# Feed-forward layers and second mixer: 2x2 block products with seven block multiplications, acts through DRAM

## The chip, the cores and the metric

The kernel runs on one core of one Trainium2 chip. The metric is the device time of one execution in microseconds (us). A profiled execution is known by its span, from its first to its last instruction. PE is the matrix engine, DVE the vector engine, ACT the scalar engine, POOL the GpSimd engine, SP the queue that issues the DMAs. PSUM is the memory that PE writes (8 banks of 512 float32 numbers per partition, a tile here is two banks), SBUF the working memory.

## The reference

Two layers on x of 1024 tokens by 1024 channels, float32. What concerns the change is what follows the first mixer: a gated feed-forward layer, the second mixer (a short convolution between two gates), and a second feed-forward layer.

```python
def mixer_c(h, w_in, conv_w, conv_b, w_out):          # w_in 1024 x 3072, w_out 1024 x 1024
    bg, cg, v = jnp.split(h @ w_in, 3, axis=-1)
    return (bg * causal_dwconv(cg * v, conv_w, conv_b)) @ w_out

def conv_ffn(h, w_gate, w_up, conv_w, conv_b, w_down): # w_gate, w_up 1024 x 2816, w_down 2816 x 1024
    g = causal_dwconv(h @ w_gate, conv_w, conv_b)      # 3 taps over the tokens
    return (jax.nn.silu(g) * (h @ w_up)) @ w_down
# around each: h = rms_norm(x, g_pre) * (1 + sc) + sh ;  x = x + (1 + gm) * rms_norm(y, g_post)
```

The vectors sc, sh and gm come from `mod = silu(c) @ mod_w[i] + mod_b[i]`, whose weights stream through the kernel too.

## The kernel before

Every product is done in three passes of a shortened float32 format: an operand x is kept as hi + lo, and a product is hi·hi + hi·lo + lo·hi. A pass over a 128x128 stationary tile and 512 moving columns is one matmul.

*Stages.* First the first mixer (recurrence and attention), to about 1177 us. Then `rest` (L1226): feed-forward layer 0, the second mixer, feed-forward layer 1. All weights come as units of 128x1024 in one fixed stream (L58) through three SBUF buffers `w_st`; `w_pump` (L172) splits each into `w_hi` (ACT cast, L209) and `w_lo` (two POOL subtractions of 512 columns, L211 through the helper at L146), five units deep. Units of `mod_w` are not split: DVE adds each into a sum (L249).

*Up products.* `proj` (L332) multiplies one unit (128 output features, 8 tiles of 128 input channels) with h^T, kept as `hh` and `hl` for two halves of 512 tokens: 8 x 3 x 2 = 48 matmuls into a two-bank PSUM tile. A feed-forward feature tile takes two units, gate and up; `gate_post` (L1302) makes the three-tap convolution (ACT L1306, two DVE operations L1308 that read PSUM), Silu (L1309), the product with up (L1311) and the split of the act (ACT L367, POOL L146). The second mixer takes three units for each tile of 128 channels.

*Output products.* After two feature tiles a `chunk` (L1246) multiplies their acts with two units of the output weights: for each of 8 token tiles 2 x 3 x 2 = 12 matmuls (`down`, L343), and DVE adds PSUM into y (L359). So up and output products alternate. The last chunk (L1279) takes four feature tiles, 24 matmuls for a token tile; each token tile is followed by `bnd1` (L301): two norms (ACT squares, POOL power L298), the residual on DVE (L308, L309), the store, and y normed on ACT (L313).

*Between layers.* `to_h` (L315) transposes y on PE (L321), applies the modulation (DVE L323) and splits h (ACT L325, then POOL or DVE L329 in turn). One half of the tokens is made inside the last chunk; `pre_half` (L1259) then runs the first two units on that half, 48 matmuls, while the other half is made.

*Order.* Each engine runs its instructions in one fixed order. It is set at build by a planner that starts from the written order and a modelled timeline (L1495); the trace shows transposes and products of different units put between each other at the layer borders.

Of the kernel before, what the change touches and what calls it, by code (L numbers as in the profile page):

```python
# [57 lines left out]
def _unit_order():  # L58
# [24 lines left out]
    def ffn(i, mods):  # L83
        for c in range(NF // 2 + 1):
            if c < NF // 2:
                for f in (2 * c, 2 * c + 1):
                    order.extend([("fg", i, f), ("fu", i, f)])
                    if mods:
                        order.append(mods.pop(0))
            if c == NF // 2:  # L90
                order.extend(mods)
                order.extend(("fd", i, f) for f in range(NF - 4, NF))
            elif 0 < c < NF // 2 - 1:
                order.extend([("fd", i, 2 * c - 2), ("fd", i, 2 * c - 1)])
                if mods:
                    order.append(mods.pop(0))
# [3 lines left out]
    for c in range(5):  # L100
        if c < 4:
            for j in (2 * c, 2 * c + 1):
                for k in (1, 2, 0):
                    order.append(("sc", 8 * k + j))
                    if mods:
                        order.append(mods.pop(0))
        if c in (1, 2):
            order.extend([("sco", 2 * c - 2), ("sco", 2 * c - 1)])
        if c == 4:
            order.extend(("sco", j) for j in range(4, 8))  # L110
# [11 lines left out]
def _is_raw(u):  # L122
    return u[0] in ("mod", "modk", "lru")
# [6 lines left out]
class K:  # L130
# [6 lines left out]
    # ------------------------------------------------------------ helpers  # L137
# [13 lines left out]
    # ------------------------------------------------------------ weight stream  # L151
# [20 lines left out]
    def w_pump(self, ahead):  # L172
        """issue loads and splits up to `ahead` units past the next one to be used"""
        upto = min(len(UNITS), self.w_next + ahead)
        while True:
# [12 lines left out]
            while self.w_split_n < upto and self.w_split_n < self.w_dma_n:  # L188
# [8 lines left out]
                hi = self.p_w.tile([128, 1024], FR, name="w_hi", bufs=self.nw)  # L197
                lo = self.p_w.tile([128, 1024], FR, name="w_lo", bufs=self.nw)
# [64 lines left out]
    def mods_here(self, limit=99):  # L263
        """the modulation units that come next in the stream"""
# [36 lines left out]
    def bnd1(self, tt, rowG, src, dst, x, last=False):  # L301
        """the residual after a layer, x = src + rstd(y) y G, goes to dst; y becomes rstd(x) x"""
# [3 lines left out]
        y = self.y[:, tt, :]  # L306
# [8 lines left out]
    def to_h(self, src, half, A, B, tmp, ks=range(8)):  # L315
        """h^T (hi, lo) of 4 token tiles from their normed tiles src(tt): A and B are columns"""
        nc = self.nc
        for k in ks:
            ps = self.ps1()
            for q in range(4):  # L320
                nc.tensor.transpose(ps[:, q * 128:(q + 1) * 128], src(4 * half + q)[:, k * 128:(k + 1) * 128], self.ident)  # L321
            hf = tmp()
            nc.vector.tensor_scalar(hf, ps, A[:, k:k + 1], B[:, k:k + 1], op0=OP.mult, op1=OP.add)  # L323
            hh, hl = self.hh[half][:, k, :], self.hl[half][:, k, :]
            nc.scalar.copy(hh, hf)  # L325
            if k % 2:
                self.pool_sub(hl, hf, hh.bitcast(FT))
            else:
                nc.vector.tensor_tensor(hl, hf, hh.bitcast(FT), op=OP.subtract)  # L329
# [13 lines left out]
    def down(self, tt, ws, acts, ps):  # L343
        """ps[:, half, :] = sum over the chunk's feature tiles of a^T[:, tt]^T W"""
        n, last = 0, 3 * len(ws) - 1
        s = slice(tt * 128, (tt + 1) * 128)
        for (ah, al), (hi, lo) in zip(acts, ws):
            for st, mv in ((ah, hi), (ah, lo), (al, hi)):
                for h in range(2):
                    self.nc.tensor.matmul(ps[:, h, :], st[:, s], mv[:, 4 * h:4 * h + 4, :],  # L350
                                          start=(n == 0), stop=(n == last))
                n += 1

    def y_add(self, tt, ps):
        nc = self.nc
        y = self.y[:, tt, :]
# [1142 lines left out]
```

## Time and profile before

| | |
|---|---|
| three runs | 3044.17, 3044.5, 3047.75 us; median 3044.5 |
| profiled execution | span 3045.4 us; no other time of its own is given |
| mean granted TensorE clock | 0.978 of full speed |
| PE busy | 2887.9 us, 95% of the span, 13329 matmuls |
| DVE, ACT, POOL busy | 1515.7, 1124.4, 1158.7 us (50%, 37%, 38%) |
| DMA | 278.48 MB, queue share 28% |

A busy time is a sum over the span; what limits a stage is read from that stage's own windows. A matmul row shows its own duration (0.39 us), but matmuls overlap: the pace is the distance from one start to the next. In a timeline row "x2" merges two instructions, and the bracket gives the idle time before it and who ended it.

### The profile page before, as it was taken

To read this page: it belongs to the slowest core of one execution; us is meant where nothing else is said; L and a number is where in the kernel's file an instruction comes from. 1 tells how busy PE (TensorE), PEld (TensorE's weight loads), DVE (VectorE), ACT (ScalarE), POOL (GpSimd) and SP (SyncE) were. 2 spreads that over 40 slices of the span, in tenths; PEclk is the share of its full clock that TensorE was granted. 3 is DMA by queue.
4 is the path that set the end of the run, shared out by engine and by line. 5 is a ranking of instruction groups with operands and counts; after the bars stand their busy time and mean duration, and the time that the engine had idled before them with its cause. 6 is when DMAs were issued, how large, how long until landed. Compare 5 with 4: busy or idle time off the path is not lost. (4 is left out here: it accounts for less than half of the span.)

```text
span 3045.4 us, 34769 instructions
## 1 busy us (share of the span) xinstructions
PE 2887.9 (95%) x13329; PEld 2370.0 (78%) x13329; DVE 1515.7 (50%) x2471; ACT 1124.4 (37%) x1681; POOL 1158.7 (38%) x978
## 2 busy tenths in 40 slices
PE   6998889898999898999999999899998999999998
PEld 4786777677878776888888888688887888888887
DVE  7749754587989897233233323721336132222224
ACT  5422166676666675321212113412134211211122
POOL 5334365544343444423232323632235323232322
PEclk9999999899999999999999999999999999999999
DMA  6456732413131322212122112422323211111113
GB/s 228 148 169 181 193 116 94 138 39 104 40 106 43 100 82 90 83 63 82 64 83 69 49 42 90 159 83 70 104 97 125 76 49 49 49 49 42 56 42 111
DMA packets 117623, 278.48 MB, mean 91 GB/s; under 512 B 10320, under 2 KB 56528, under 8 KB 117328
## 3 DMA queue, kind: packets, MB, share of 16 engines
q1 hardware_dynamic: 117456, 276.26, 28.0%
q8 instruction: 105, 1.72, 0.2%
q14 instruction: 62, 0.51, 0.1%
HBM read 226.93 MB, written 49.28 MB: 91 GB/s over the span
## 5 line engine op out<-in xcount | busy, mean ns | idle before, releaser
L146 POOL TENSOR_TENSOR w_lo<-w_st,w_hi 128x512 fp32r<-128x512 f32 x440 | 595.2, 1377 | 1273.2 <-ACT w_hi L209 1256.6
L339 PE MATMUL mm<-hh,w_hi 128*128 128x512 f32 x2336 | 734.8, 394 | 22.5 <-ACT t L900 12.3
L339 PE MATMUL mm<-hl,w_hi 128*128 128x512 f32 x2336 | 734.2, 392 | 1.7 <-POOL hl L146 1.4
L339 PE MATMUL mm<-hh,w_lo 128*128 128x512 f32 x2336 | 732.1, 391 | 0.0
L209 ACT CAST w_hi<-w_st 128x1024 fp32r<-128x1024 f32 x220 | 230.6, 1050 | 1139.6 <-PE mm L339 693.6
L339 PEld LDWEIGHTS mm<-hh,w_hi 128*128 128x128 f32 x2336 | 441.5, 190 | 117.4 <-ACT t L900 14.2
L339 PEld LDWEIGHTS mm<-hl,w_hi 128*128 128x128 f32 x2336 | 442.3, 189 | 95.0 <-POOL hl L146 1.7
L339 PEld LDWEIGHTS mm<-hh,w_lo 128*128 128x128 f32 x2336 | 441.7, 189 | 92.6
L1308 DVE SCALAR_TENSOR_TENSOR acc<-mm,colt,acc 128x1023 f32<-128x1023 f32 x88 | 112.8, 1282 | 440.1 <-ACT acc L1306 438.5
L359 DVE TENSOR_TENSOR y<-mm,y 128x1024 f32<-128x1024 f32 x160 | 195.3, 1223 | 212.6 <-PE mm L350 212.6
L350 PE MATMUL mm<-w_hi,ah 128*128 128x512 f32 x832 | 257.0, 390 | 0.6 <-DVE y L359 0.6
L350 PE MATMUL mm<-w_lo,ah 128*128 128x512 f32 x832 | 256.4, 389 | 0.0
L350 PE MATMUL mm<-w_hi,al 128*128 128x512 f32 x832 | 256.0, 389 | 0.0
L1122 ACT CAST pth<-t 128x512 fp32r<-128x512 f32 (+1 forms) x260 | 146.4, 585 | 100.3 <-PE t L1120 87.4
L350 PEld LDWEIGHTS mm<-w_hi,al 128*128 128x128 f32 x832 | 156.2, 188 | 32.6
L350 PEld LDWEIGHTS mm<-w_lo,ah 128*128 128x128 f32 x832 | 156.2, 188 | 32.5
L350 PEld LDWEIGHTS mm<-w_hi,ah 128*128 128x128 f32 x832 | 155.6, 188 | 32.9 <-DVE y L359 1.1
L249 DVE SCALAR_TENSOR_TENSOR macc<-w_st,cact,macc 128x1024 f32<-128x1024 f32 x70 | 97.4, 1391 | 166.7 <-DMA w_st<-in_wu_dram 166.6
L1311 DVE TENSOR_TENSOR m<-acc,mm 128x1024 f32<-128x1024 f32 x44 | 53.7, 1222 | 230.4 <-PE mm L339 226.7
L1128 DVE TENSOR_TENSOR ptl<-t,pth 128x512 fp32r<-128x512 f32 x228 | 152.1, 684 | 14.6 <-ACT pth L1122 13.3
L146 POOL TENSOR_TENSOR al<-m,ah 128x1024 fp32r<-128x1024 f32 x52 | 125.6, 2415 | 13.7 <-ACT ah L367 13.7
L298 POOL TENSOR_TENSOR rs_r<-rs_v,mhalf 128x1 f32<-128x1 f32 x64 | 63.4, 992 | 149.4 <-DVE rs_v L296 142.7
(260 smaller groups left out, 3878.3 us busy)
## 6 DMA issues: line engine op xcount, KB each, us to landing
w_st<-in_wu_dram SPq DMA_DIRECT2D x317, 512.0 KB, 3.3
acc<-d_x SPq DMA_DIRECT2D x24, 512.0 KB, 3.3
d_x<-acc SPq DMA_DIRECT2D x17, 512.0 KB, 2.7
d_q<-t SPq DMA_DIRECT2D x32, 256.0 KB, 3.8
k<-d_k SPq DMA_DIRECT2D x16, 512.0 KB, 7.7
q<-d_q SPq DMA_DIRECT2D x32, 256.0 KB, 3.0
d_rn<-t SPq DMA_DIRECT2D x16, 512.0 KB, 3.3
rn<-d_rn SPq DMA_DIRECT2D x64, 128.0 KB, 2.7
```

Source lines behind the costliest of these rows:

```text
L146: self.nc.gpsimd.tensor_tensor(out, a, b, op=OP.subtract)
L209: self.nc.scalar.copy(hi, st)
L249: nc.vector.scalar_tensor_tensor(self.macc, st, self.cact[:, k:k + 1], self.macc, op0=OP.mult, op1=OP.add)
L298: nc.gpsimd.tensor_tensor(r, v, self.mhalf, op=OP.pow)
L339: self.nc.tensor.matmul(ps[:m, h, :], st[:, k, :m], mv[h][:, k, :], start=(n == 0), stop=(n == 23))
L350: self.nc.tensor.matmul(ps[:, h, :], st[:, s], mv[:, 4 * h:4 * h + 4, :], start=(n == 0), stop=(n == last))
L359: nc.vector.tensor_tensor(y, p, y, op=OP.add)
L1122: nc.scalar.copy(hi[:m], ps[:m])
L1128: nc.vector.tensor_tensor(lo, ps, hi.bitcast(FT), op=OP.subtract)
L1308: nc.vector.scalar_tensor_tensor(acc[:, s:], X[:, :T - s], cw(2 - s), acc[:, s:], op0=OP.mult, op1=OP.add)
L1311: nc.vector.tensor_tensor(m, acc, flat(psu), op=OP.mult)
```

## The change

Only `rest` and what it calls change; the first mixer keeps its code (its weight tiles get a pool of their own, `wx`, freed after the attention).

A gate and an up unit, (or two units of the second mixer) form a pair. The pair's weights are a 2x2 block matrix A (row 1 the first unit, row 2 the second; columns the two halves of the input channels), h^T is a 2x2 block matrix B (rows the channel halves, columns the token halves). The four blocks of the result come from seven block products of 12 matmuls with 512 columns, 84 for a pair in place of 96. The sums S1 to S4 of weight blocks (DVE) and T1 to T4 of h blocks are formed, and then split into hi and lo, as are A11, A12, A22, B11, B21 and B22. Products are summed into two PSUM banks in turn, and between the products ACT or DVE read a bank's state (e1 to e7).

The output products no longer stand between the up products. A finished act goes unsplit to DRAM (`d_act`); when all of a layer's acts are done, `out_phase` loads them, splits them (ACT, POOL) and runs all chunks, each of two feature tiles, the last one too. At a layer border the first token half gives B11 and B21; the products p1 and p2 of the first two pairs run on it; `h_second` then makes B22 and T1 to T4.

```diff
-    return u[0] in ("mod", "modk", "lru")
+    return u[0] in ("mod", "modk", "lru", "fg", "fu", "fd", "sc", "sco")
...
+        def wsplit(src):
+            hi, lo = p_x.tile([128, 512], FR, name="xh", bufs=10), p_x.tile([128, 512], FR, name="xl", bufs=10)
+            nc.scalar.copy(hi, src)
+            self.pool_sub(lo, src, hi.bitcast(FT))
+            return hi, lo
+        def pair_jobs(ph, u1, u2):     # 7 jobs, a yield after each
+            self.mods_here()
...
+            S12, S34 = w_tile(ph, 0, "S12"), w_tile(ph, 1, "S34")
...
+            tt(S1, a21, a22, op=OP.add)
+            tt(S2, S1, a11, op=OP.subtract)
+            wt[u1, "S2"] = wsplit(S2)
+            tt(S4, a12, S2, op=OP.subtract)
+            tt(S3, a11, a21, op=OP.subtract)
...
+        def h_second(ph, th, AB):
+            new_blocks(("B22", "T1", "T2", "T3", "T4"))
...
+            for k in range(4):
+                ps = self.psbig()
+                trans(ps[:, 0, :], th, k)
+                trans(ps[:, 1, :], th, k + 4)
...
+                affine(x12, ps[:, 0, :], AB, k)
+                affine(x22, ps[:, 1, :], AB, k + 4)
+                bsplit("B22", k, x22)
+                sub(z3, x22, x12)
+                sub(x12, x12, h("B11", 0))
+                sub(x12, x12, h("B11", 1))
+                bsplit("T1", k, x12)
+                sub(z, x22, x12)
+                bsplit("T2", k, z)
+                bsplit("T3", k, z3)
+                sub(x12, h("B21", 0), z)
+                add(x12, x12, h("B21", 1))
+                bsplit("T4", k, x12, True)
...
+        class Pair:                    # a and c are the two banks of s.ps
+                s.steps = iter((s.p1, s.e1, s.p2, s.e2, s.p6, s.e6, s.p5, s.e5, s.p7, s.e7, s.p3, s.e3, s.p4, lambda: None))
...
+            p1: s.prod(0, "A11", "B11", True)    e1: nc.scalar.copy(s.G1, s.a)
+            p2: s.prod(1, "A12", "B21", True)    e2: nc.vector.tensor_tensor(s.G1, s.c, s.G1, op=OP.add)
+            p6: s.prod(0, "S2", "T2", False)     e6: nc.scalar.copy(s.G2, s.a)
+            p5: s.prod(1, "S1", "T1", True)      e5: nc.scalar.copy(s.U, s.c)
+            p7: s.prod(0, "S3", "T3", False)     e7: nc.vector.tensor_tensor(s.U, s.a, s.U, op=OP.add)
+            p3: s.prod(1, "S4", "B22", False)    e3: nc.vector.tensor_tensor(s.G2, s.c, s.G2, op=OP.add)
+            p4: s.prod(0, "A22", "T4", False)
...
+            for n, p in enumerate(ps):           # up_phase, after the early products
+                while p.left:
+                    jobs_upto(min(at + 10, end + 8))
+                    p.step()
+                    at += 1
...
+                post(n, p)
...
+        def act_load(d, f):
+            t = slot(f % 14, "act")
+            nc.sync.dma_start(t[:, 1, :].bitcast(FT), d[f])
+            nc.scalar.copy(t[:, 0, :], t[:, 1, :].bitcast(FT))
+            self.pool_sub(t[:, 1, :], t[:, 1, :].bitcast(FT), t[:, 0, :].bitcast(FT))
...
+            def post(f, p):                      # feed-forward
+                conv(acc, p.G, ...)
+                nc.scalar.activation(acc, acc, AF.Silu)
+                nc.vector.tensor_tensor(a1, a1, p.a, op=OP.mult)
+                nc.vector.tensor_tensor(a2, a2, p.U, op=OP.mult)
+                nc.sync.dma_start(d[f], acc)
```

In the block above the methods p1 to p4 and e1 to e7 are written one to a line; `conv` is the ACT Identity with scale and bias and the two DVE operations of before, now on `G` in SBUF. `post_sc` does the same for the second mixer with its two gates. The modulation units move to places between the pairs and the output units.

## Rows read from the trace of the kernel before

**Rows 1.** The page: busy us, share of the span and instructions of each engine.
```profile
PE 2887.9 (95%) x13329; PEld 2370.0 (78%) x13329; DVE 1515.7 (50%) x2471; ACT 1124.4 (37%) x1681; POOL 1158.7 (38%) x978
```

**Rows 2.** Windows by stage: us, busy (x instructions) of PE, PEld, DVE, ACT, POOL; clock; DMA.
```profile
1177.00:1216.00 39.00, 32.36 (x155) 25.53 (x154) 27.65 (x33) 16.53 (x24) 21.08 (x15) 0.87 0.34 118
1216.00:1870.00 654.00, 654.00 (x2899) 541.72 (x2898) 196.59 (x159) 143.01 (x135) 207.35 (x144) 1.00 0.20 67
...
1912.00:1960.00 48.00, 36.86 (x175) 29.47 (x174) 41.22 (x46) 25.39 (x37) 32.94 (x22) 0.89 0.49 174
1960.00:2245.00 285.00, 285.00 (x1267) 236.09 (x1266) 80.06 (x66) 61.50 (x59) 89.38 (x62) 1.00 0.26 87
...
2287.00:2335.00 48.00, 38.16 (x177) 30.68 (x176) 37.88 (x43) 25.85 (x38) 31.57 (x23) 0.86 0.41 148
2335.00:2985.00 650.00, 650.00 (x2873) 538.29 (x2873) 170.68 (x137) 140.68 (x133) 205.00 (x144) 1.00 0.16 52
```

**Rows 3.** Timeline of PE: first and last of 97 double rows; then first products on one half.
```profile
1239.70 0.62 PE L339 MATMUL mm<-hh,w_lo 128*128 128x512 f32 x2
...
1283.22 0.62 PE L339 MATMUL mm<-hh,w_lo 128*128 128x512 f32 x2
...
1935.87 0.39 PE L339 MATMUL mm<-hh,w_hi 128*128 128x512 f32 x1
...
1937.90 0.39 PE L339 MATMUL mm<-hl,w_hi 128*128 128x512 f32 x1
```

**Rows 4.** Groups by line and shape, 1216 to 3046 us, DVE, ACT and POOL.
```profile
L359 DVE TENSOR_TENSOR y<-mm,y 128x1024 f32<-128x1024 f32 x160 | 195.3, 1223 | 212.6 <-PE mm L350 212.6
L249 DVE SCALAR_TENSOR_TENSOR macc<-w_st,cact,macc 128x1024 f32<-128x1024 f32 x47 | 65.5, 1393 | 132.2 <-DMA w_st<-in_wu_dram 132.1
L1308 DVE SCALAR_TENSOR_TENSOR acc<-mm,colt,acc 128x1023 f32<-128x1023 f32 x44 | 56.4, 1283 | 438.5 <-ACT acc L1306 438.5
L323 DVE TENSOR_SCALAR m<-mm,rowc,modc 128x512 f32<-128x512 f32 x32 | 24.9, 802 | 8.5 <-PE mm L321 8.5
L1306 ACT ACTIVATE acc<-mm,colt 128x1024 f32<-128x1024 f32 x44 | 52.7, 1198 | 0.0
L1309 ACT ACTIVATE acc<-acc 128x1024 f32<-128x1024 f32 x44 | 46.7, 1061 | 116.7 <-DVE acc L1308 116.7
L325 ACT CAST hh<-m 128x512 fp32r<-128x512 f32 x32 | 19.7, 618 | 23.8 <-DVE m L323 23.2
L146 POOL TENSOR_TENSOR w_lo<-w_st,w_hi 128x512 fp32r<-128x512 f32 x318 | 413.1, 1324 | 1093.7 <-ACT w_hi L209 1093.7
```

**Rows 5.** Timeline of DVE and POOL: half-width operations alone, then both engines together.
```profile
1175.53 0.69 DVE L1012 TENSOR_TENSOR y<-dn,y 128x512 f32<-128x512 f32 x1 [0.50 <-PE dn L1022]
1205.66 0.68 DVE L329 TENSOR_TENSOR hl<-m,hh 128x512 fp32r<-128x512 f32 x1
...
1930.52 2.31 DVE L309 SCALAR_TENSOR_TENSOR acc<-y,rs_r,acc 128x1024 f32<-128x1024 f32 x1
1931.71 3.97 POOL L146 TENSOR_TENSOR hl<-m,hh 128x512 fp32r<-128x512 f32 x2
1932.75 1.77 DVE L329 TENSOR_TENSOR hl<-m,hh 128x512 fp32r<-128x512 f32 x1
```

**Rows 6.** Timeline of the border after layer 0's feed-forward: last chunk's first matmuls, last normed token tile.
```profile
1874.75 0.70 PE L350 MATMUL mm<-w_hi,ah 128*128 128x512 f32 x2
...
1943.95 0.69 PE L321 MATMUL mm<-colt,y 128*128 128x128 f32 x2 [5.11 <-ACT y L313]
```

**Rows 7.** Timeline of the end: the last matmuls, the last addition, gain product and residual.
```profile
3035.43 0.61 PE L350 MATMUL mm<-w_hi,al 128*128 128x512 f32 x2
...
3036.34 1.22 DVE L359 TENSOR_TENSOR y<-mm,y 128x1024 f32<-128x1024 f32 x1
...
3038.90 1.22 DVE L308 TENSOR_TENSOR y<-y,macc 128x1024 f32<-128x1024 f32 x1
3040.56 1.28 DVE L309 SCALAR_TENSOR_TENSOR acc<-y,rs_r,acc 128x1024 f32<-128x1024 f32 x1 [0.44 <-POOL rs_r L298]
```

More of the change, by code (lines that the diff above doesn't have):

```diff
@@ L399, in run @@
         self.d_rn = self.p_d.tile([8, 128, 2, T], FT, name="d_rn")
+        self.d_act = [self.p_d.tile([n, 128, T], FT, name=f"d_act{i}") for i, n in enumerate((NF, 8, NF))]
         es_h, es_kv = ExitStack(), ExitStack()
@@ L403, in run @@
         es_h.close()
-        p_y = ctx.enter_context(self.pool("y", side="right"))
-        self.y = p_y.tile([128, NT, D], FT, name="y")
+        self.p_y = ctx.enter_context(self.pool("y", side="right"))
+        self.y = [self.y_tile(tt) for tt in range(NT)]
         with ExitStack() as es:
@@ new lines, in all_jobs, with jobs_upto, job_count @@
+        def all_jobs():
+            for n, us in enumerate(phases()):
+                for u in us:
+                    for _ in (out_jobs(u) if n % 2 else pair_jobs(n, *u)):
+                        yield n
+        jobs = all_jobs()
+        done = [0, 0]
+        def jobs_upto(n):
+            while done[0] < n and next(jobs, None) is not None:
+                done[0] += 1
+        def job_count(n):
+            return sum((2 if m % 2 else 7) * len(us) for m, us in enumerate(phases()[:n]))
@@ new lines, in rest, with __init__, step, early @@
+        class Pair:
+            def __init__(s, ph, u, n, ts):
+                s.ph, s.u, s.n, s.ts = ph, u, n, ts
+                s.steps = iter((s.p1, s.e1, s.p2, s.e2, s.p6, s.e6, s.p5, s.e5, s.p7, s.e7, s.p3, s.e3, s.p4, lambda: None))
+                s.left = 7
+            def step(s):
+                next(s.steps)()
+                next(s.steps)()
+                s.left -= 1
+            def early(s):
+                s.p1()
+                s.p2()
+                s.steps = iter((lambda: (s.e1(), s.e2()), s.p6, s.e6, s.p5, s.e5, s.p7, s.e7, s.p3, s.e3, s.p4, lambda: None))
+                s.left = 5
+            def late(s):
+                next(s.steps)()
+            def prod(s, bank, w, b, start):
+                wh, wl = (x.rearrange("p (k n) -> p k n", n=128) for x in wt.pop((s.u[0], w)))
+                bh, bl = hb[b]
+                n = 0
+                for k in range(4):
+                    for st, mv in ((wh, bh), (wh, bl), (wl, bh)):
+                        nc.tensor.matmul(s.ps[:, bank, :], st[:, k, :], mv[:, k, :], start=start and n == 0, stop=n == 11,
+                                         skip_group_check=True)
+                        n += 1
+            def p1(s):
+                s.ps = self.psbig()
+                s.a, s.c = s.ps[:, 0, :], s.ps[:, 1, :]
+                s.prod(0, "A11", "B11", True)
+            def e1(s):
+                s.G = w_tile(s.ph, 4 + s.n % 2, "G")
+                s.G1, s.G2 = (s.G[:, half(h)] for h in s.ts)
+                nc.scalar.copy(s.G1, s.a)
+            def p2(s):
+                s.prod(1, "A12", "B21", True)
+            def e2(s):
+                nc.vector.tensor_tensor(s.G1, s.c, s.G1, op=OP.add)
+            def p6(s):
+                s.prod(0, "S2", "T2", False)
+            def e6(s):
+                nc.scalar.copy(s.G2, s.a)
+            def p5(s):
+                s.prod(1, "S1", "T1", True)
+            def e5(s):
+                s.U = w_tile(s.ph, 2 + s.n % 2, "U")[:, :512]
+                nc.scalar.copy(s.U, s.c)
+            def p7(s):
+                s.prod(0, "S3", "T3", False)
+            def e7(s):
+                nc.vector.tensor_tensor(s.U, s.a, s.U, op=OP.add)
+            def p3(s):
+                s.prod(1, "S4", "B22", False)
+            def e3(s):
+                nc.vector.tensor_tensor(s.G2, s.c, s.G2, op=OP.add)
+            def p4(s):
+                s.prod(0, "A22", "T4", False)
@@ new lines, in up_phase @@
+        def up_phase(ph, ts, post, first, extra):
+            us = phases()[ph]
+            base = job_count(ph)
+            end = job_count(ph + 1)
+            ps = [Pair(ph, u, n, ts) for n, u in enumerate(us)]
+            jobs_upto(base + 9)
+            ps[0].early()
+            ps[1].early()
+            first()
+            ps[0].late()
+            ps[1].late()
+            at = base + 4
+            for n, p in enumerate(ps):
[3 more added lines that the diff above has]
+                    at += 1
+                    if n == len(ps) - 1:
+                        extra(7 - p.left)
+                post(n, p)
```

354 lines of the change are left out of this document (183 added, 171 removed).

## The prediction

> **What bounds the kernel now.** I read the page first: PE is busy for 2887.9 of 3045.4 us [rows 1], but that is a mean over stages, so the windows come next. In the three long stages after the first mixer (feed-forward 0, second mixer, feed-forward 1) PE is busy for the whole window at clock 1.00, while DVE, ACT and POOL stand at 22 to 32% and the DMAs at 0.16 to 0.26 [rows 2]. Only PE bounds these 1590 us. At the three borders between them PE loses 6.6, 11.1 and 9.8 us of idle time, and the clock falls to 0.86 to 0.89, some 4 to 5 us more each: about 11, 15 and 15 us lost [rows 2]. Third, the pace: 97 double rows lie 43.52 us apart from first to last, 96 steps, so two matmuls take 0.4533 us and one 226.7 ns. The products on one token half, which change the stationary tile at every matmul and write one bank, as all products of the change will, start 9 steps in 2.03 us, 226 ns apart [rows 3]. So the new products run at the old pace.
>
> **Removed matmuls.** There are 22 + 12 + 22 = 56 pairs, each with 84 matmuls for 96: 672 fewer, by 226.7 ns **-152.3 us**. The output products keep their 2496.
>
> **The pairs.** A pair now lasts 84 x 0.2267 = 19.04 us on PE, a product 2.72. Beside it stand:
> - POOL: 7 weight splits by 1.32 = 9.3 us [rows 4].
> - ACT: 7 casts by 0.62, three PSUM copies priced alike, Identity 1.20, Silu 1.06: 8.5 us [rows 4].
> - DVE: 4 sums of weight blocks by 0.68, three additions from PSUM and two gate products by 0.69 [rows 5], two convolution steps by 1.28, at most one modulation unit by 1.39 [rows 4]: 10.1 us (in the second mixer two such units in most pairs, but no gate product after the convolution).
>
> Each fits, but not independently. When a POOL subtraction runs, DVE operations that read two SBUF tensors wait for it: L309 takes 2.31 us and L329 1.77, against 0.68 for L329 alone, and POOL's pair takes 3.97 [rows 5] where two take 2.65 [rows 4]. I count such operations of the two engines one after the other: 4 x 0.68 + 2 x 1.28 + 0.69 + 1.39 = 7.4 for DVE (the convolution now reads G in SBUF, not PSUM) plus 9.3 for POOL, 16.7 of 19.04 us. It fits at 88%.
>
> What can stop PE is the order inside a pair. Product p6 goes on in the bank that e1 must have copied, and all of PE is queued behind it; likewise e2 for p5, e6, e5, e7 for p7, p3, p4. Each has one product, 2.72 us, for a copy of 0.6 to 0.7. The longest way to one of them: after p3, e3 (0.69), Identity (1.20), two convolution steps (2.57), Silu (1.06), and behind Silu in ACT's queue the next pair's e1 (0.62): 6.1 us. It has p4, p1 and p2, 8.2 us: 2.0 to spare. If each convolution step meets a whole POOL operation (2 x 1.32) and Identity a cast (0.62), it is 3.3 late against 2.0: 1.3 us of stall in a pair, 72 us in 56. At the mean, POOL is busy 49% of a pair, a half operation of 0.66 left, so 0.3 for each step and 0.3 for the cast: 0.9, which is covered. Bounds 0 and 72; nothing here makes PE quicker than its pace, so none below zero. I take 0.2 us for a pair, **+11**, near the lower end, since the long stages show no PE idle at all behind their own chains [rows 2].
>
> Weight splits run 9 products ahead (ten buffers), 24 us; the act's store waits on SP for the last gate product, and the weight loads behind it serve splits a pair later. The DMAs gain 52 acts twice by 0.5 MB on stages that use a quarter of them [rows 2]. All this I cost at nothing; without cover a late load would show as PE waiting for a weight split.
>
> **The borders.** The second token half now costs more than a split. Before, 8 tiles: 8 affines and 8 splits. Now for each of 4 k: two affines (0.80, from PSUM [rows 4]), seven DVE operations on two SBUF tensors (0.68 [rows 5]) and four POOL splits (1.32 [rows 4]). DVE alone: 6.4 us per k. One after the other with POOL: 4.8 + 5.3 = 10.0 us per k. p6 needs T2 of all four k: at the first price it waits about 3 x 6.4 + 5 = 24 us, at the second 3 x 10 + 8 = 38. I take 38, as rows 5 show the engines taking turns.
>
> The Trainium skill says the same (SBUF — State Buffer, "SBUF: two separate sides"): the port pair of VectorE and GpSimd is an exclusive lock held for a whole instruction, against a VectorE operation with two SBUF inputs. By that rule the border is the 38 us; with ports that merely shared a bandwidth it would lie between the two. The trace agrees: 1.77 for 0.68.
>
> The last chunk is halved too: 12 matmuls, 2.72 us, for a token tile where DVE needs 1.22 + 1.22 + 1.28 = 3.7 [rows 4, 7]. From its start: first tile 2.7, DVE 30, the first half's h 9.1 (8 x 0.80 + 4 x 0.68), a last norm about as long as the 4.2 us from the last addition to the last residual at the end [rows 7]: the last y is normed near 46 us. (Before, 69.2 us after the start [rows 6], with 43.5 us of matmuls in it.) By then PE has done 21.8 us of output products and some 5 of transposes: 19 lost. In the next 38 us PE has the early products p1, p2 of two pairs (48 matmuls, 10.9), transposes (3) and those parts of p6 and p5 whose k are there (about 8): 16 lost. With 2 for a slower clock after the gap: 37 us lost, against 15, so +22 at two borders. At the first border no chunk stands before: 6.6 as now, 27 of the 38 beyond p1 and p2, 2 for the clock, 36 against 11: +25. Together **+69**. Lower bound, with DVE and POOL side by side (24 for 38): +27. Upper, if the 7 weight splits and 4 sums of the first pair (12 us) stand ahead on the same engines at each border: +105.
>
> **The end.** The last chunk at DVE's 3.7 us a tile in place of PE's 2.72: 8 x 1.0 = **+8**.
>
> **Entry of the output stages.** The first acts are stored, loaded and split inside the last pair (asked for after p2 and p5). I take a microsecond or so of wait at each of three: **+4**, bounds 0 and 12. The chunks themselves keep 21.8 us of PE against 9.8 of DVE.
>
> **Sum.** -152.3 + 11 + 69 + 8 + 4 = -60. On the span of 3045.4 that is 2985; the median of the runs lies 0.9 below the span, which I neglect. Forecast 2985 us. Bounds: 3045.4 - 152 + 27 + 8 = 2928 and 3045.4 - 152 + 72 + 105 + 8 + 12 = 3090.
>
> **Rivals.**
> - *The borders are hidden.* The planner puts second-half work beside the last chunk, and DVE and POOL overlap: borders +27, no stall in pairs, about 2930. For it: the trace shows transposes and products of several units put between each other at a border. Against: both engines' bare work grows there. Chance 0.22 (2915 to 2955).
> - *The shared port sets the pair (slower).* Place: e1 and e2 of every pair. DVE's convolution waits for POOL's subtractions, ACT's Silu waits in front of e1, and p6 stops. Price 1.3 us in each of 56 pairs, 72 for my 11, and the same turns with the first pair's splits ahead at the borders, +105 for +69: 3082. The pairs alone take it to 3046; it decides from (60 + 11) / 56 = 1.3 us of stall per pair, or 0.6 with the borders. For it: 88% on one port, and waits on the way to e1. Against: 12% spare, and 2.0 us to spare in a chain that loses 0.9 in the mean. Chance 0.13.
> - *Seven products don't save an eighth*, because PE pauses at each of the 392 product changes: 0.15 us at each would take 60 and end where it is now, 3045. Against: the change from one unit to the next shows no pause in stages of 100% [rows 2]. Chance 0.05.
>
> **Chances.** Forecast, 2955 to 3025: 0.57. Hidden borders 0.22, shared port 0.13, no saving 0.05, quicker than 2915 by a cause not seen 0.03. A measurement here tells 0.2%, some 6 us, from no change. Faster 0.82, same 0.05, slower 0.13. Leaving out the slower cases and the lower part of the hidden borders, the range is 2930 to 3045; the forecast's own is 2955 to 3025.
>
> **What would show it.** PE matmul count 672 lower at the same 226.7 ns; PE busy all through the middle of the up stages, or waits of p6 and p5 on e1 and e2 (ACT copy, DVE addition of 512 columns); at each border one PE gap whose releaser is the split of T2 (POOL), with DVE and POOL in turns; DVE, not PE, in turn with the last chunk's token tiles. I am wrong if up stages show PE below 95% or if a border loses under 25 or over 50 us.

## The result: slower by 2.4%, and the profile after

The changed kernel takes 3118.2 us (median of 4 runs, 3114.9 to 3122.0) where the kernel before takes 3045.1 beside it (3044.2 to 3047.8): a ratio of 1.024, 95% interval 1.023 to 1.026. I had forecast 2985, with a range up to 3045. The profiled execution has a span of 3113.1 us, 67.7 above that of before.

The page's first part, as in [rows 1]:

```profile
PE 2793.9 (90%) x12657; PEld 2263.1 (73%) x12657; DVE 1971.6 (63%) x3007; ACT 1346.5 (43%) x2209; POOL 1505.5 (48%) x1182
```

The 672 matmuls are gone (13329 to 12657), as forecast. PE is busy for 94 us less, but the span has grown: PE waits more. Where, the windows of the changed kernel say (columns as in [rows 2]; in order: border 1, pairs of feed-forward 0, its output stage, border 2, pairs of the second mixer, border 3, pairs of feed-forward 1, and 100 us inside these):

```profile
1177.00:1260.00 83.00, 50.35 (x193) 36.97 (x192) 71.18 (x73) 32.59 (x56) 64.78 (x42) 0.73 0.15 51
1260.00:1690.00 430.00, 411.68 (x1796) 334.11 (x1795) 241.02 (x253) 183.17 (x265) 242.32 (x154) 1.00 0.36 123
1690.00:1890.00 200.00, 200.00 (x884) 165.64 (x883) 85.70 (x70) 34.74 (x50) 73.45 (x49) 1.00 0.22 75
1890.00:2040.00 150.00, 99.65 (x386) 75.71 (x385) 116.20 (x125) 64.30 (x103) 84.33 (x60) 0.75 0.24 88
2040.00:2250.00 210.00, 191.15 (x824) 153.33 (x822) 122.10 (x123) 68.41 (x107) 108.43 (x72) 0.98 0.37 132
...
2310.00:2470.00 160.00, 110.98 (x438) 84.55 (x437) 116.04 (x131) 67.44 (x108) 92.46 (x62) 0.77 0.24 86
2470.00:2860.00 390.00, 383.28 (x1682) 315.34 (x1682) 196.14 (x216) 170.13 (x249) 216.19 (x146) 1.00 0.30 106
...
2600.00:2700.00 100.00, 100.00 (x443) 82.81 (x442) 52.86 (x63) 43.47 (x64) 51.78 (x37) 1.00 0.23 84
```

Where PE does not wait it keeps its pace: 443 matmuls in 100 us are 226 ns each [rows 3]. In the three border windows PE is idle for 33 to 50 us, and the granted clock falls to 0.73 to 0.77 (0.86 to 0.89 before [rows 2]). The pairs of feed-forward 0 and of the second mixer, which were to be full, have 18 and 19 us of idle PE.

To compare kernels I keep one account. A stretch's loss is its length less 0.2267 us for each 512-column matmul that starts in it [rows 3], of whichever stage, and 0.11 for each transpose of y (their median distance from start to start); idle time and lower clock both count as loss. A border runs from the start of the last four feature tiles' output products (border 1 from the first mixer's last product) to the end of the first 168 products of the next stage, the pairs from there to their stage's last product, an output stage to the next border or to the end. The planner puts up to 96 output products between the products of a stage's pairs; they count where they run. The columns behind the first are experiments told below: last4 has four feature tiles in the last chunk, mods out no modulation units among the pairs, wsplit act and wsplit DVE the weights' lo parts on ACT or (with last4) on DVE, three and both combine changes, mods early moves the second mixer's modulation units in both.

| us lost | changed | last4 | mods out | wsplit act | three | wsplit DVE | both | mods early |
|---|---|---|---|---|---|---|---|---|
| three borders | 46, 68, 70 | 48, 53, 52 | 46, 70, 70 | 47, 65, 63 | 32, 44, 42 | 48, 48, 52 | 38, 40, 40 | 38, 40, 40 |
| pairs ffn 0, mixer, ffn 1 | 28, 26, 11 | 35, 27, 10 | 37, 10, 3 | 9, 24, 1 | 11, 26, 1 | 12, 23, 2 | 11, 24, 3 | 10, 15, 4 |
| three output stages | 1, 9, 0 | 2, 10, 1 | 16, 0, 18 | 0, 9, 0 | 1, 10, 2 | 1, 9, 3 | 10, 3, 4 | 10, 1, 4 |
| end | 25 | 10 | 25 | 25 | 9 | 10 | 9 | 9 |
| all | 285 | 249 | 294 | 243 | 177 | 208 | 181 | 171 |
| median of runs | 3118.2 | 3082.1 | 3126.0 | 3073.7 | 3010.9 | 3035.2 | 3010.1 | 3005.0 |

By the same account the kernel before lost 62 us from the first mixer's last product on (12, 16, 16 at the borders, 9 in the stages between, 10 at the end). So 223 more are lost against 152 saved, and the stages start 3 us earlier: 67.7.

**The residual loop.** DVE in the last chunk of feed-forward 0, one token tile to the next (timeline; start, duration, last bracket the idle time and its releaser):

```profile
1913.72 1.28 DVE L301 SCALAR_TENSOR_TENSOR x<-y,rs_r,x 128x1024 f32<-128x1024 f32 x1 [0.44 <-POOL rs_r L290]
1914.93 1.21 DVE L334 TENSOR_TENSOR y<-mm,y 128x1024 f32<-128x1024 f32 x1
...
1917.46 0.15 DVE L288 TENSOR_SCALAR rs_v<-rs_v 128x1 f32<-128x1 f32 x1 [1.03 <-ACT junk L287]
1917.54 1.21 DVE L300 TENSOR_TENSOR y<-y,macc 128x1024 f32<-128x1024 f32 x1
1919.19 1.28 DVE L301 SCALAR_TENSOR_TENSOR x<-y,rs_r,x 128x1024 f32<-128x1024 f32 x1 [0.44 <-POOL rs_r L290]
```

In the middle of the chunk the residuals L301 lie 5.47 us apart, though DVE's large operations take 3.7. DVE waits 1.03 for ACT's square of y, which stands behind the square of x, and 0.44 for POOL's power. The old last chunk had 24 matmuls, 5.44 us, for a tile, and hid just this loop; now there are 2.72. The last token tile is normed (ACT) only here:

```profile
1955.67 1.15 ACT L305 ACTIVATE y<-x,rs_r 128x1024 f32<-128x1024 f32 x1 [2.62 <-POOL rs_r L290]
```

**The end.** Behind the last feed-forward no x is normed again, and another loop shows. The last rows are of the chain that ended last, then one of DVE:

```profile
3091.02 4.97 DMA out_dram<-x
...
3096.01 4.14 DMA x<-d_x
```
```profile
3105.92 1.28 DVE L301 SCALAR_TENSOR_TENSOR x<-y,rs_r,x 128x1024 f32<-128x1024 f32 x1 [4.36 <-DMA x<-d_x]
```

There are two buffers for x: the load of a token tile's x waits until the result of the tile two before it is stored, 5.0 us for the store and 4.1 for the load here. DVE waits 8.4 us for such loads in all.

**The turns at a border.** Border 2, second half of the tokens: DVE, then POOL, then PE:

```profile
1961.95 1.53 DVE L1327 TENSOR_SCALAR hx<-mm,rowc,modc 128x512 f32<-128x512 f32 x2
...
1981.23 0.68 DVE L1343 TENSOR_TENSOR hx<-B,hx 128x512 f32<-128x512 f32 x1
1981.84 1.88 DVE L1343 TENSOR_TENSOR hx<-hx,B 128x512 f32<-128x512 f32 x3
1983.75 1.64 DVE L1343 TENSOR_TENSOR hx<-hx 128x512 f32<-128x512 f32 x1
1985.32 1.75 DVE L1318 TENSOR_TENSOR T<-hx,T 128x512 fp32r<-128x512 f32 x1
```
```profile
1980.84 4.01 POOL L138 TENSOR_TENSOR B<-hx,B 128x512 fp32r<-128x512 f32 x1 [0.78 <-ACT B L1316]
1984.81 5.84 POOL L138 TENSOR_TENSOR T<-hx,T 128x512 fp32r<-128x512 f32 x4
```
```profile
1990.70 0.80 PE L1393 MATMUL mm<-T,xh 128*128 128x512 f32 x1 [2.48 <-POOL T L138]
1998.86 0.80 PE L1393 MATMUL mm<-T,xh 128*128 128x512 f32 x1 [6.94 <-ACT T L1316]
```

A 512-column operation on two SBUF tensors takes 1.64 and 1.75 us on DVE (0.68 alone [rows 5]), one on POOL 4.01 while DVE starts five beside it, four of which keep 0.6 to 0.7. PE has not one gap here but four behind one another that end with a part of T, two with POOL's lo and two with ACT's hi; by the written order of the products (p6 first) that is T2, as forecast, but the last and longest (6.94) waits for ACT.

Before the second half starts, PE has already run 35 of the 48 products p1 and p2 of the first two pairs. From 1961.95 to 1998.86 it runs 23 products and 24 transposes, and loses 29 of these 37 us; 34 of border 2's 68 are lost up to the last normed y (1956.82).

**The turns in the pairs.** Groups by line and shape from 1177 us on (convolution steps, weight splits), then four rows of DVE and PE in feed-forward 0:

```profile
L138 POOL TENSOR_TENSOR xl<-S,xh 128x512 fp32r<-128x512 f32 x224 | 329.6, 1477 | 260.3 <-ACT xh L1236 256.6 <-PE mm L1393 3.6
L1476 DVE SCALAR_TENSOR_TENSOR acc<-G,colt,acc 128x1022 f32<-128x1022 f32 x52 | 97.3, 1871 | 0.4
L1476 DVE SCALAR_TENSOR_TENSOR acc<-G,colt,acc 128x1023 f32<-128x1023 f32 x52 | 89.4, 1720 | 30.4 <-ACT acc L1474 30.1
```
```profile
1433.25 0.69 DVE L1254 TENSOR_TENSOR S<-w_st 128x512 f32<-128x512 f32 x1 [1.72 <-DMA w_st<-in_wu_dram]
...
1435.06 1.78 DVE L1255 TENSOR_TENSOR S<-S,w_st 128x512 f32<-128x512 f32 x1
1436.76 0.68 DVE L1411 TENSOR_TENSOR G<-mm,G 128x512 f32<-128x512 f32 x1
```
```profile
1437.50 0.73 PE L1393 MATMUL mm<-T,xh 128*128 128x512 f32 x2 [1.25 <-DVE G L1411]
```

The convolution steps, 1.28 us when they read PSUM [rows 4], take 1.72 and 1.87 in the mean now that both tensors lie in SBUF (one of them took 10.60, see the last section; without it the 1.72 is 1.55). A weight sum that meets a POOL subtraction takes 1.78; e2 (L1411) stands behind it in DVE's queue, and PE behind e2 stops for 1.25 us. e2 itself, one tensor in PSUM, keeps its 0.68: it is late, not slow.

The first row shows a second part of that lateness: the pair's first weight sum stood 1.72 us for its unit's load, and DVE's order with it. By these numbers e2 would have held PE for 0.15 us at most without this wait, or without the 1.1 us of the collision. Of the ten waits of 0.8 us and more on e2 in feed-forward 0 seven have both ahead of them, two have only collisions, one only a late load (3.71 us, of a modulation unit). The loads themselves wait for one of the three buffers, which POOL's subtractions of the raw blocks free (138.1 us of such waits for 33 loads, 1266 to 1650 us).

### The profile page after: what moved, and what is told of

It is laid out like the page before. It is cut to its first block, busy times and chain, and to the rows that moved or that the text cites. A ratio compares the mean times of both kernels' runs of the same rounds, so it can differ in the third digit from the quotient of the medians.

```text
span 3113.1 us, 35733 instructions
## 1 busy us (share of the span) xinstructions
PE 2793.9 (90%) x12657; PEld 2263.1 (73%) x12657; DVE 1971.6 (63%) x3007; ACT 1346.5 (43%) x2209; POOL 1505.5 (48%) x1182
## 3 DMA queue, kind: packets, MB, share of 16 engines
q8 instruction: 100, 1.64, 0.2%
## 5 line engine op out<-in xcount | busy, mean ns | idle before, releaser
L1393 PE MATMUL mm<-T,xh 128*128 128x512 f32 x1792 | 575.7, 402 | 94.7 <-ACT T L1316 29.0
L138 POOL TENSOR_TENSOR xl<-w_st,xh 128x512 fp32r<-128x512 f32 x272 | 381.2, 1414 | 477.0 <-ACT xh L1236 473.9
L1393 PEld LDWEIGHTS mm<-T,xh 128*128 128x128 f32 x1792 | 343.0, 193 | 187.3 <-ACT T L1316 33.8
L326 PE MATMUL mm<-xh,act 128*128 128x512 f32 x1664 | 450.5, 391 | 5.2 <-DVE y L334 4.1
L1393 PE MATMUL mm<-B,xh 128*128 128x512 f32 x1344 | 428.3, 400 | 27.5 <-DVE hf L1327 8.1
L1393 PE MATMUL mm<-T,xl 128*128 128x512 f32 x896 | 357.0, 398 | 3.1 <-POOL xl L138 3.0
L138 POOL TENSOR_TENSOR w_lo<-w_st,w_hi 128x512 fp32r<-128x512 f32 x112 | 167.0, 1514 | 176.8 <-ACT w_hi L201 160.0
L315 PE MATMUL mm<-hh,w_hi 128*128 128x512 f32 x544 | 174.3, 402 | 17.4 <-ACT t L883 12.1
L315 PE MATMUL mm<-hh,w_lo 128*128 128x512 f32 x544 | 171.7, 397 | 0.0
L315 PE MATMUL mm<-hl,w_hi 128*128 128x512 f32 x544 | 171.6, 397 | 0.0
```

The lines of the kernel that those rows point to most:

```text
L138: self.nc.gpsimd.tensor_tensor(out, a, b, op=OP.subtract)
L315: self.nc.tensor.matmul(ps[:m, h, :], st[:, k, :m], mv[h][:, k, :], start=(n == 0), stop=(n == 23))
L326: self.nc.tensor.matmul(ps[:, h, :], a[:, st, s], w[h][mv], start=(n == 0), stop=(n == last))
L1393: nc.tensor.matmul(s.ps[:, bank, :], st[:, k, :], mv[:, k, :], start=start and n == 0, stop=n == 11, skip_group_check=True)
```

## The experiments

Theory L is the residual loop at the borders and the end; theory P is POOL and DVE taking turns on SBUF, in pairs and at borders; theory M, the rival in the pairs, is modulation units in DVE's queue. All ratios are against the kernel before on the same chip.

### Four feature tiles in the last chunk again

```diff
-            last = len(us) // 2 - 1
+            last = len(us) // 2 - 2
-                fs = (2 * c, 2 * c + 1)
+                fs = (2 * c, 2 * c + 1) if c < last else tuple(range(2 * c, 2 * c + 4))
```


> One size changed: the last chunk of each output stage takes four feature tiles again, 24 matmuls for a token tile, in place of two. Theory L (a loop): in the changed kernel one token tile of the last chunk costs 5.5 us whatever PE does, because its addition to y, square (ACT), power (POOL) and residual (DVE) follow one another and hold DVE's order; 24 matmuls (5.44 us) fill that loop. Then about 20 us come back at each of the two borders and at the end: 3118 - 60 = 3058 us, with the rows of the residual still 5.5 us apart. Rival (the prediction's): DVE's bare work of 3.7 us a tile sets the pace and the rest of a border is the second half's h: 8 us come back at each of three places, 3094.

Measured: 3082.1 us, ratio 1.011 (1.009 to 1.013), 36 less. Borders 2 and 3 and the end lose 15, 18 and 15 less, 47 together (60 expected in the time); border 1, which has no chunk ahead of it, does not move. At the borders that is theory L: the residuals still lie 5.47 us apart. At the end they lie 5.42 apart, near PE's 5.44 for 24 matmuls, and none waits for a load of x any more; so what came back there is the loop over the two buffers of x, not that of theory L. The pairs of feed-forward 0 lose 7 more.

### No modulation units among the pairs

All units of the pairs go to the output stages.

```diff
-            if mods and f > 0:
-                order.append(mods.pop(0))
...
-            if mods:
-                order.append(mods.pop(0))
+            for _ in range(3 if f < 4 else 2):
+                if mods:
+                    order.append(mods.pop(0))
...
-    ffn(0, mod(0, 5) + mod(1, 1, 0))
-    mods = mod(1, 2, 4, 3)
+    ffn(0, mod(0, 5) + mod(1, 1, 0) + mod(1, 2, 4, 3))
+    mods = []
...
```

> One thing moved: no modulation unit stands between pairs any more; the 48 of the first two up stages go between the output units of feed-forward 0, the 8 of the last between those of feed-forward 1. Theory M: PE's stalls inside the pairs (about 24 us in feed-forward 0, 20 in the second mixer, next to none in feed-forward 1 once its modulation units are through) come from these units, which stand in DVE's queue waiting for their weights and hold one of three load buffers; and two of them hold up the second border. Then 40 to 50 us come back: about 3073. Rival: the stalls come from DVE and POOL taking turns over conv steps and weight splits; with one operation of 1.4 us fewer for a pair, about 10 come back: 3108.

Measured: 3126.0 us, 1.026 (1.024 to 1.028): both were missed. The pairs of the second mixer and of feed-forward 1 came mostly free (26 to 10 and 11 to 3 us lost); those of feed-forward 0 lost 9 more, and the two output stages into which the units went 15 and 18 more (the middle one 9 less). In feed-forward 0 the order moved the waits from e2 to e1 (PE waiting in 1266 to 1650 us, changed kernel, then this one):

```profile
PE mm L1393 <- DVE G L1411: 14.0, 10, 2.1
PE mm L1393 <- ACT G L1405: 1.7, 7, 0.4
```
```profile
PE mm L1392 <- ACT G L1404: 11.8, 10, 3.7
PE mm L1392 <- DVE G L1410: 5.7, 9, 0.6
```

Theory M falls for the pairs of feed-forward 0, the largest loss. For those of the second mixer it is borne out: without the units 16 of the 26 us went. A new order of the planner's alone can make such a difference too, but the last experiment points the same way.

### POOL's subtractions replaced by ACT copies

Two runs: in the first the lo parts of B22, T1, T2 and T3 are plain ACT copies, in the second those of all weight blocks; the matmuls stay, the results lose these parts.

```diff
-                bsplit("B22", k, x22)
+                bsplit("B22", k, x22, act=True)      # nc.scalar.copy(lo, x); and so T1, T2, T3
...
-            self.pool_sub(lo, src, hi.bitcast(FT))
+            nc.scalar.copy(lo, src)
```


> Leaves out the lo parts of B22, T1, T2 and T3: ACT writes plain copies there, so POOL has no part in the second token half. Theory P (turns on the port): the second half's h takes 42 us at a border since DVE's seven operations and POOL's four of a k exclude each other; with DVE alone it takes 4 x 6.4 = 26 and PE's last gap shrinks by about 15 at each of three borders: 3118 - 45 = 3073, the DVE rows of that stage at 0.68 us, not 1.7. Rival: the chain from DVE to ACT to POOL to PE sets it, and ACT now has 9 casts for 5 in a k: at most 5 us at a border, 3105 or more.

> Leaves out the lo parts of all weight blocks of the three layers: ACT writes plain copies there (14 casts for a pair, about 13 us of 19), POOL none. Theory P for the pairs: DVE and POOL taking turns makes the stalls inside pairs (44 us) and 9 us of each border: 3118 - 44 - 27 = 3047. Theory M: the stalls in pairs come from the modulation units' waits and stay; only the borders gain 9 each: 3091.

Measured: 3085.7 us (1.013, 1.011 to 1.015), and 3073.7 us (1.009, 1.008 to 1.011). The first takes 16, 9 and 11 us from the borders, between theory P's 45 in all and the rival's 15. The second takes 18 and 10 from the pairs of the two feed-forward layers, nearly all that they lost, and 11 from borders 2 and 3 together. It fell short of theory P's 3047, which had the whole loss of the pairs and 27 at the borders: the second mixer's pairs kept 24 of 26.

### Silu behind the next pair's e1

```diff
                     p.step()
                     at += 1
+                    if late:
+                        late()
+                        late = None
...
-                post(n, p)
+                late = post(n, p)     # returns Silu, gate products and store as a function
```


> Only the written order is changed: Silu, the two gate products and the store of a feed-forward pair are written after the first product of the next pair and its copy e1. Theory C (in the pairs the chain convolution, Silu, next e1 makes PE wait): half of the 34 us lost in the pairs of layer 0 and of the 20 us in those of layer 1 go, about 3093 us. Theory P (the waits come from DVE and POOL taking turns on SBUF, whatever stands in front of e1): the pairs keep their losses, 3110 to 3120 us.

Measured: 3123.0 us, 1.026 (1.024 to 1.027). PE's waits in 1266 to 1650 us stay: 15.4 us on e2, 3.0 on e1. The pairs lose 30, 26 and 10. Theory C, the chain of conv, Silu and e1 that I had walked through in the prediction, falls.

### The second half's splits on DVE, and the three changes together

The first keeps all parts and moves the four POOL subtractions for each k to DVE (last chunk of four as well). The second joins the chunk of four with the two sets of ACT copies.

```diff
-                bsplit("B22", k, x22)
+                bsplit("B22", k, x22, True)      # and so T1, T2, T3
```

> The last chunk has four feature tiles (3082 us alone), and the lo parts of B22 and T1 to T3 are subtracted on DVE (0.68 us) and not on POOL (1.32 us, in turns with DVE); nothing is left out. Theory P: the three borders lose 20 us less together than with the last chunk of four alone, 3062 us. Rival D (DVE is the queue that ends the border, and four more operations for each k on it take what the turns cost): 3080 us or more.

> Three earlier changes together: the last chunk of four feature tiles, and the lo parts of the weight blocks and of B22 and T1 to T3 left out (plain ACT copies in place of the POOL subtractions). Alone they gave 36, 44 and 32 us. If the residual loop and the turns of DVE and POOL are separate causes, the gains add up: 3006 us, below the kernel before. If they are one wait seen three times, the sum stops short: 3045 us or more, and something else stands behind the loss.

Measured: 3078.7 us (1.011, 1.009 to 1.013): borders lose 4, 7 and 5 less than with the chunk alone, but the pairs of feed-forward 1 lose 29 in place of 10, in the same code, whose instructions the planner put in another order. Two waits come back each 40 us, both behind an operation that had met a POOL subtraction (DVE, ACT, then PE):

```profile
2627.82 1.78 DVE L1255 TENSOR_TENSOR S<-S,w_st 128x512 f32<-128x512 f32 x1
2629.52 0.68 DVE L1411 TENSOR_TENSOR G<-mm,G 128x512 f32<-128x512 f32 x1
2630.12 2.37 DVE L1476 SCALAR_TENSOR_TENSOR acc<-G,colt,acc 128x1022 f32<-128x1022 f32 x1
```
```profile
2632.58 1.06 ACT L1482 ACTIVATE acc<-acc 128x1024 f32<-128x1024 f32 x1 [2.53 <-DVE acc L1476]
2633.55 0.57 ACT L1405 COPY G<-mm 128x512 f32<-128x512 f32 x1
```
```profile
2630.25 0.73 PE L1393 MATMUL mm<-T,xh 128*128 128x512 f32 x2 [0.63 <-DVE G L1411]
2634.17 0.73 PE L1393 MATMUL mm<-B,xh 128*128 128x512 f32 x2 [0.89 <-ACT G L1405]
```

Each wait (0.6 and 0.9 us) is smaller than the extra 1.1 us of the operation in front of it. That is why one order of the same pairs shows waits and another none: it depends on which sum or step meets POOL ahead of e1 or e2.

The three together: 3010.9 us, 0.989 (0.987 to 0.991). Alone they gave 36, 32 and 44; together 107 of 113. So the last chunk's size and the turns are separate causes, and without both (and without those lo parts) the kernel is 34 us quicker than the one before.

### The second half's affines on ACT, then two passes

Both have the chunk of four and all second-half splits on DVE; the first adds the modulation on ACT and the late Silu, the second the modulation on ACT and an order that makes T2 of all four k before T3 and T4.

```diff
-                affine(x12, ps[:, 0, :], AB, k)
+                aff_act(x12, ps[:, 0, :], AB, k)      # ACT Identity with scale and bias from AB
...
                 sub(z, x22, x12)
                 bsplit("T2", k, z, True)
+                bsplit("B22", k, x22, True)
+            for k in range(4):
...
+                sub(z3, z, h("B11", 0))
+                sub(z3, z3, h("B11", 1))
                 bsplit("T3", k, z3, True)
```

> Last chunk of four, the splits of the second half on DVE, its modulation (two for each k) on ACT in place of DVE, and the late Silu; nothing is left out. Theory P with C: 3062 less about 6 us of DVE at each of three borders, less 25 us in the pairs: about 3019 us, below the kernel before. Rival (ACT, with the hi casts and the modulation, becomes the queue that ends the border, and the pairs keep their waits): 3055 us or more.

> Last chunk of four, modulation of the second half on ACT, all its splits on DVE, and these in two passes: B22, T1 and T2 of all four k first, then T3 and T4. Nothing is left out. Theory B (at the border PE waits for T2 of the last k behind T3 and T4 of the earlier ones): T2 is there after 24 DVE operations of 0.69, 16.5 us, where the one-pass form took 26; 10 us less at each border, 3040 us. Rival (p7 and p4 then wait for T3 and T4 as long as p6 did for T2, the sum of DVE work being the limit): 3065 us or more.

Measured: 3070.1 us (1.008, 1.005 to 1.010) and 3064.3 us (1.006, 1.004 to 1.008). Both theories' times, 3019 and 3040, were missed. The borders lose 39, 43 and 44, and 40, 44 and 44: the two passes gave nothing there. They also cost one more DVE operation for each k (z3 takes two subtractions in place of one), 2.7 us at a border, less than the 10 expected. So theory B's gain didn't come: T2's place behind T3 and T4 isn't what sets the border.

### Weight splits on DVE, alone and with the rest

Now nothing is left out: POOL's seven subtractions for each pair go to DVE, whose queue grows by 4.8 us for each pair.

```diff
-            self.pool_sub(lo, src, hi.bitcast(FT))
+            nc.vector.tensor_tensor(lo, src, hi.bitcast(FT), op=OP.subtract)
```


> Last chunk of four feature tiles (3082 us alone), and the lo parts of all weight blocks subtracted on DVE (0.69 us) in place of POOL (1.28 us, in turns with DVE); nothing is left out. Theory P: without a POOL operation in the pairs a weight sum or a convolution step no longer takes 1.8 to 2.4 us, e1 and e2 come in time, and of the 86 us that PE loses in the pairs some 50 go: 3032 us. Rival D (seven more operations for each pair bring DVE to about 15 of 19 us, and in its fixed order e2, e7 and e3 stand behind them): 3080 us or more.

> The two changes before together: no POOL subtraction in pairs or in the second half, two passes, last chunk of four. Theories P and B add up: about 2990 us, below the kernel before. Rival D (DVE, now with every subtraction, is the bound in pairs and at the border): 3045 us or more.

Measured: 3035.2 us (0.996, 0.994 to 0.997) and 3010.1 us (0.988, 0.986 to 0.989). Both are quicker than the kernel before. The first lands near theory P's 3032, in part by luck: by the account the pairs lose 37 in place of 72, 35 us less and not 50, and all stages together 41 less; its first mixer was 5 us shorter in the profiled execution, in code that is the same. The second missed its 2990. The first's convolution steps and PE's waits in 1266 to 1650 us:

```profile
L1476 DVE SCALAR_TENSOR_TENSOR acc<-G,colt,acc 128x1023 f32<-128x1023 f32 x52 | 70.9, 1363 | 20.8 <-ACT acc L1474 20.7
L1476 DVE SCALAR_TENSOR_TENSOR acc<-G,colt,acc 128x1022 f32<-128x1022 f32 x52 | 68.4, 1315 | 0.1
```
```profile
PE mm L1393 <- ACT G L1417: 3.1, 1, 3.1
PE mm L249 <- DVE macc L241: 1.1, 1, 1.1
PE mm L1393 <- DVE G L1411: 0.9, 1, 0.9
```

The steps are back near 1.3 us, and 15.7 us of waits on e1 and e2 (16.4 with the chunk of four alone) have become 0.9. DVE does 2161.6 us of work, where the changed kernel had 1971.6, and PE waits less for it. DVE's waits of a weight sum for a load, 18.4 us in the changed kernel there, are gone too: without POOL the buffers come free in time. So this edit takes away both parts of e2's lateness and doesn't tell them apart; the pairs of feed-forward 1 in the 3078.7 us run (2585 to 2760 us), where no sum waits for a load and PE still loses 7.6 us on e1 and e2, show the collisions alone. The pairs of the two feed-forward layers lose 12 and 2 us now, those of the second mixer still 23.

### The modulation units of the second mixer three to a pair

```diff
-            if c + us[0] > 8:
-                order.extend(mods.pop(0) for _ in range(2))
+            if c + us[0] > 8 and mods:
+                order.extend(mods.pop(0) for _ in range(3))   # eight pairs, none in the last three
```


> The kernel of the last chunk of four, two passes and no POOL subtraction in pairs or second half (3010 us), with the 24 modulation units of the second mixer's stage placed three to a pair from its second pair on, so that they end three pairs before the stage does; before, two to a pair until its end. Theory W (the 24 us that this stage loses in every version are modulation units in DVE's queue whose weights land late, when the loads of the first acts share the DMAs): the waits at the stage's end, about 10 us, go: 3000 us. Rival (DVE has 15 us of 19 in such a pair with two units, 18 or more with three, and e2, e7 and e3 come late in eight pairs): 3010 us or more.

Measured: 3005.0 us, 0.986 (0.984 to 0.988). PE's waits from 2150 to 2250 us, without and with this edit:

```profile
PE mm L1405 <- DVE U L1442: 6.3, 1, 6.3
PE mm L1405 <- DVE G L1448: 1.6, 1, 1.6
PE mm L249 <- DVE macc L241: 0.9, 1, 0.9
```
```profile
PE mm L1405 <- DVE U L1442: 0.8, 1, 0.8
PE mm L249 <- DVE macc L241: 0.3, 1, 0.3
```

The wait at the stage's end goes, and pairs and output stage of the mixer together lose 16 us in place of 27; the mean granted clock of these pairs is 1.00 in place of 0.98. The interval of the time overlaps that of the run without the edit (it was on another chip), so the gain in time is indicated, not shown.

## Why the prediction was wrong, step by step

- **Removed matmuls, -152:** right, in number and pace. The rival that product changes cost a pause falls with it: 443 matmuls in 100 us.
- **The pairs, +11: mis-sized.** They lose 65, 1.2 us for each. The price stood in the prediction as the upper bound, 1.3 us, 72 together, and its rival "the shared port sets the pair" named the mechanism. I took 0.2 because the long stages of before showed no idle PE. But those had POOL subtractions beside a DVE that read PSUM; the change moved the convolution's input to SBUF and added sums on SBUF, so they were no evidence for the lower end. I also priced a mean (half a POOL operation a step), where a fixed order makes the same bad meeting recur in pair after pair. The place was partly wrong too: more often e2 behind a weight sum than e1 behind Silu, and with the late Silu nothing changed. Taking the weight splits off POOL brought the pairs from 72 to 37 (chunk of four in both), those of feed-forward 0 and 1 from 45 to 14. Not all of the 65 is that mechanism, so it is in part luck that the bound of 72 comes near it. The second mixer's 26 hardly moved when POOL was taken out (23), but fell to 10 without modulation units among the pairs and, in the best version, from 24 to 15 with the units moved. I had priced such a unit by DVE's 1.39 us and all loads at nothing. A late load was to show as PE waiting for a weight split; it shows as DVE waiting ahead of e2, in feed-forward 0 too (18.4 us before weight sums). From 2028 to 2298 us of the changed kernel DVE waits 21.6 us for the weights of these units.
- **The borders, +69: measured +141, the largest miss.** Forecast 37, 37, 36 us lost; measured 46, 68, 70, against 12, 16, 16 before. My own sign of being wrong, over 50 at a border, came at two of three. The second half's turns were priced about right: 38 forecast, and 37 from DVE's first operation on it (1961.95) to the end of PE's last long gap (1998.86). What failed stands on both sides of them. I gave a token tile of the last chunk DVE's 3.7 us of work; the loop over DVE, ACT, POOL and DVE takes 5.47. So the last y was normed about 61 us after the chunk's start, not 46, and with the chunk of four 15 and 18 us came back. DVE starts on the second half only 5 us after that norm, which I took as nothing. And I had about 8 us of p6 and p5 run beside the turns: 10 such products did, 2 us. With no turns and that chunk the borders lose 38 to 40. That this is near my 37 is chance: the 37 was for a border with the turns.
- **The end, +8: measured +15,** but not by DVE's 3.7 us a tile: DVE waits for loads of x that wait for stores. I hadn't priced the two buffers of x. With the chunk of four the loss is 10, as before.
- **Entry of the output stages, +4:** the three stages lose 11 in all, 9 of them in the second mixer's. There PE waits 6.7 us once, for a modulation sum and not for an act:

```profile
PE mm L249 <- DVE macc L241: 6.7, 1, 6.7
```

Sum as measured: -152 + 65 + 141 + 15 + 11 = +80; the kernel before lost 9 us in its stages that my terms took as nothing, and the start is 3 us earlier, which gives the 68 of the spans.

The Trainium skill (SBUF — State Buffer, "SBUF: two separate sides") says that DVE and GpSimd hold their common port pair as an exclusive lock for a whole instruction. The rows agree, also where I had not applied it: a weight sum took 0.68 alone and 1.78 against POOL, a convolution step 1.3 and, in the mean, 1.72 and 1.87, and e2, which reads PSUM, didn't change. I had used that rule at the border and a mean in the pairs.

What stays open: why a border still loses 38 to 40 us in the best version against 12 to 16 before. At its border 2 (both) 8 us go between the last output product and the last normed y, 9 from there to the second half's first operation, and 22 in the second half, where DVE is busy for 35.15 of 36.56 us (columns as in [rows 2]):

```profile
1925.63:1962.19 36.56, 21.65 (x81) 14.52 (x79) 35.15 (x56) 21.40 (x37) 2.11 (x1) 0.72 0.07 26
```

So in that second half DVE's own work is the limit, now without turns; a version with less of it wasn't tried, nor one with more buffers for x. The 17 us ahead of it, and the 14 that the feed-forward pairs still lose, I haven't taken apart. Nor was a fourth load buffer tried, which would tell the late loads of feed-forward 0 from the collisions.

## What to carry to other kernels

Before moving an operand from PSUM to SBUF on DVE, count what POOL does beside it: a POOL operation that lies under DVE's two-tensor operations costs both, and giving POOL's work to DVE (seven subtractions, 4.8 us for each pair) was worth 47 us of the median here (41 by the account) although DVE was already the busier. Price a token loop by its period from start to start in the trace, not by one engine's busy time, and count the buffers that its loads and stores share; the loop that another stage hides is the first thing to show when that stage is halved. And where the order is fixed, price a collision at its full size in each repetition, not at its mean.

## What the runs showed of the hardware

- The same pairs lost 10 or 29 us by the planner's order alone (feed-forward 1, chunk of four, without and with an edit that doesn't touch the pairs): a single edit's effect on a stage can be some 20 us of order.
- The turns cost both engines: POOL's subtraction of 512 columns took 1.25 us at the shortest and 1.48 in the mean of the S blocks, and another one 4.01 beside five DVE operations.
- An operation that loses can lose many times in a row: a convolution step that takes 1.3 us alone took 10.60 in the pairs of feed-forward 1, while POOL ran six subtractions without a pause (to 2849.62), and ended 1.1 us after the last of them. PE then waited 4.65 us for e3, which stands behind it.

```profile
2840.09 10.60 DVE L1476 SCALAR_TENSOR_TENSOR acc<-G,colt,acc 128x1023 f32<-128x1023 f32 x1 [1.31 <-ACT acc L1474]
```
```profile
2838.78 2.42 POOL L138 TENSOR_TENSOR act<-act 128x1024 fp32r<-128x1024 f32 x1
...
2848.36 1.26 POOL L138 TENSOR_TENSOR xl<-w_st,xh 128x512 fp32r<-128x512 f32 x1
```
